# Holding back the first step of a gather until stages of another chain are done

## The chip, the cores and the metric

The kernel runs on one core of a Trainium2 chip. TensorE multiplies matrices, VectorE and ScalarE work elementwise, GpSimd (POOL in the profile) issues the indirect gathers, and SyncE (SP) issues most loads. The metric is the time of one execution in microseconds (us); of several runs the median is given. Lower is better.

## What is computed

A decoder block over 512 tokens with a model width of 1024: a normalized input goes through two token mixers in parallel (attention and a recurrent mixer, RWKV-7), their outputs are merged by gates, and the result goes through a channel mixer that picks 128 of 16384 experts for each token.

```python
h = modulate(rms_norm(x, norm_mix), sh1, sc1)
mix = token_mixer(h, ...)            # (g_mla * o_mla + g_rwkv * o_rwkv) @ w_out
x = x + gt1 * mix
h = modulate(rms_norm(x, norm_ffn), sh2, sc2)
# peer_ffn: top 16 of two lists of 128 keys for each of 8 heads, top 16 of their sums
act = gelu(einsum('bpd,bphkd->bphk', h, expert_down[expert_idx]))
x = x + gt2 * einsum('bphk,bphkd->bpd', gates * act, expert_up[expert_idx])
```

In the recurrent mixer each head's output is normalized over its 64 channels (the group norm of the title's chain), gets a bonus term, and is multiplied by a gate.

## The kernel before

The 512 tokens are four blocks of 128 rows. They go through the block's stages in three groups: block 0, block 1, and blocks 2 and 3 together; this third one is the last group. The code is a set of generators that emit instructions; a list scheduler then fixes one order for each engine, by a simulated time and a priority (`tc.cur_priority`), and on the chip each engine works through its order without leaving it. An engine that waits for one instruction holds up all that stand behind it.

The channel mixer is done in two ways. For blocks 0 and 1 it is done by **gathers**, in `peer()`: 128 per block, 256 in all. Gather number s fetches, for each of the 128 tokens, one expert's row of `expert_down` and one of `expert_up` into a tile gl of 128 x 2048 (1.05 MB; L1116, issued by GpSimd; four gl buffers, GL). VectorE's first step (L1119) multiplies gl's lower half with the token's row h2p and adds up into z. ScalarE takes gelu(z) and multiplies it with the gate (L1120, L1121). VectorE's second step (L1125) adds z times gl's upper half to acc. The second step frees the gl buffer, and only then can the gather four numbers later be issued. At the end of a block acc is multiplied and added with two rows e (L1131, L1132) and stored to out (L1133, issued by SP); the next block then loads h2p (L1109) and clears acc on GpSimd (L1111), and both have a single buffer. The gathers are emitted at the back of the priority (LATE), so the scheduler puts them into gaps.

For blocks 2 and 3 all experts are computed **densely**. Their chain, the last group's, is: `rwkv_out` (the group norm from the reduce m, L879, to y*m, L887; the transposition into ps_ynT, L893; bonus and gate, L903 and L904, up to the two products yT, L906), `tail_b` (ps_m = w_o times yT on TensorE, then Gr and Mg on VectorE, L953 and L954), `tail_c` (ps_mix = Mg times w_out; t_mix and x, L977 and L978; the norm of the rows and x*rs, L986; the transposition into ps_h2T, L991; h2T and its split hh and hl, L1148 and L1149; then ps_q = h2T times w_q and the top-16 search, from L1014), the selection, `dense_spread` (o and og, L1234 and L1237, build the gate matrix, which goes through the memory tile gd and comes back as G), and the dense loop of 128 iterations. An iteration splits u_raw and v_raw into high and low parts (uh, ul, vh, vl, L1148 and L1149), computes ps_z and accumulates into acc on TensorE (a PSUM tile of the same name as the gathers' acc), and multiplies act with G (L1287). At its end y = acc * gt + x2e (L1310, L1311) is stored to out.

The gathers run beside the last group's chain, the spread and the dense loop, and use the same VectorE, ScalarE and DMA engines.

Of the kernel before, what the change touches and what calls it, by code (L numbers as in the profile page):

```python
# [2 lines left out]

# [5 lines left out]
F32 = mybir.dt.float32  # L10
# [6 lines left out]
ALU = mybir.AluOpType  # L17
AX = mybir.AxisListType

P = 128  # L20
T = 512
D = 1024
# [12 lines left out]
LATE = 1000  # L35
ZLATE = 100
ZFIRST = 20
AZ = 32
PZ = 8
NG = 3  # L40
# [113 lines left out]
def _build(ctx, tc, nc, A, out):  # L154
# [309 lines left out]
    for ct in range(4):  # L464
        st = sp.tile([P, 2, 64], F32, name="st", tag="st", bufs=8)
        G.memset(st, 0.0)
        state.append(st)

    def norm(x, junk):

# [404 lines left out]
    def rwkv_out(cts, nb, R, y2, sg, yT):  # L875

        yv = y2.rearrange("p d (h c) -> p (d h) c", h=2)
        m, m2_, m3 = small("m", 4), small("m2", 4), small("m3", 4)
        V.tensor_reduce(m, yv, axis=AX.X, op=ALU.add)  # L879
        V.tensor_scalar(m, m, 1.0 / 64, None, op0=ALU.mult)  # L880
        V.tensor_tensor(yv, yv, bc(m, 64, 2), op=ALU.subtract)
        j = fin("jv", [P, 4, 64])
        S.activation(j, yv, AF.Square)
        V.tensor_reduce(m2_, j, axis=AX.X, op=ALU.add)
        V.tensor_scalar(m2_, m2_, 1.0 / 64, None, op0=ALU.mult)
        rsqrt(m3, m2_, 4, GN_EPS)
        V.tensor_tensor(yv, yv, bc(m3, 64, 2), op=ALU.mult)  # L887
        yield
        ps = psum_r("ps_ynT")
        u = fin("u", [P, 2, P])  # L890
        for d in range(2):
            ct = cts[d // nb]
            PE.transpose(ps[:, d * P:(d + 1) * P], y2[:, d], ident)  # L893
            S.activation(u[:, d], ps[:, d * P:(d + 1) * P], AF.Identity, scale=col("ln_x_w")[:, ct:ct + 1],
                         bias=col("ln_x_b")[:, ct:ct + 1])
        t = fin("bv", [P, 2, P])
        ps = psum_r("ps_bonus")
        mm(ps[:, :256], C("blk"), R["rk"])
        for d in range(2):
            mm(ps[:, 256 + d * P:256 + (d + 1) * P], w_gu[:, cts[d // nb] * P:(cts[d // nb] + 1) * P],  # L900
               sg[:, (d % nb) * P:(d % nb + 1) * P])
        yield
        V.tensor_tensor(flat(t), ps[:, :256], R["v"], op=ALU.mult)  # L903
        V.tensor_tensor(u, u, t, op=ALU.add)  # L904
        for d in range(2):
            V.tensor_tensor(yT[d % nb][:, cts[d // nb]], u[:, d], ps[:, 256 + d * P:256 + (d + 1) * P], op=ALU.mult)  # L906
        yield


# [27 lines left out]
    def tail_b(blocks, M, Gr, yT):  # L937
        nb = len(blocks)
        n = nb * P
        jn = 4 // nb  # L940
        for j0 in range(0, KT, jn):
            ps = psum_x("ps_m")
            for j in range(j0, j0 + jn):
                if j % 2 == 0:
                    w = load_w("w_o", A["w_o"][1, j // 2])
                for bb in range(nb):
                    o = ps[:, ((j - j0) * nb + bb) * P:((j - j0) * nb + bb + 1) * P]
                    for k in range(4):
                        mm(o, w[:, 4 * (j % 2) + k], yT[bb][:, k, :], k == 0, k == 3)
            pv = ps.rearrange("p (j b t) -> p b j t", j=jn, b=nb)  # L950
            for bb in range(nb):
                g, m = Gr[bb][:, j0:j0 + jn], M[bb][:, j0:j0 + jn]
                V.scalar_tensor_tensor(g, g, 1.0, pv[:, bb], op0=ALU.add, op1=ALU.mult)  # L953
                V.tensor_tensor(m, m, g, op=ALU.add)  # L954
            yield

    def tail_c(blocks, M, tops):
        nb = len(blocks)
# [22 lines left out]
        for bb, b in enumerate(blocks):  # L981
            nc.scalar.dma_start(x2d[b * P:(b + 1) * P, :], x2[bb])
            hT2 = (hTr if b in DENSE else Mh)("h2T", [P, KT, P])
            h2T.append(hT2)
            rs = norm(x2[bb], flat(hT2))
            V.tensor_scalar(x2[bb], x2[bb], rs, None, op0=ALU.mult)  # L986
            for k4 in range(2):
                ps = psum_x("ps_h2T")
                for j in range(4):
                    k = 4 * k4 + j  # L990
                    PE.transpose(ps[:, j * P:(j + 1) * P], x2[bb][:, k * P:(k + 1) * P], ident)  # L991
                for j in range(4):
                    k = 4 * k4 + j
                    S.activation(hT2[:, k], ps[:, j * P:(j + 1) * P], AF.Identity, scale=hA2[:, k:k + 1], bias=hB2[:, k:k + 1])
            if b in DENSE:
                dense_h(b, hT2)
                if b == DENSE[-1]:
                    ahead["z"] = dense_ahead()
            yield
        for bb, b in enumerate(blocks):  # L1000
# [101 lines left out]


    LAG = 1

    def peer(b, ii, gates, pl):

        h2 = pl.tile([P, D], F32, name="h2p", tag="h2p", bufs=1)
        nc.sync.dma_start(h2, h2d[b * P:(b + 1) * P, :])  # L1109
        acc = pl.tile([P, D], F32, name="acc", tag="acc", bufs=1)  # L1110
        G.memset(acc, 0.0)  # L1111
        wait = []
        for s in range(P + LAG):
            if s < P:
                gl = pl.tile([P, 2 * D], F32, name="gl", tag="gl", bufs=GL)
                G.indirect_dma_start(out=gl, out_offset=None, in_=A["experts"],  # L1116
                                     in_offset=bass.IndirectOffsetOnAxis(ap=ii[:, s:s + 1], axis=0))
                z = pl.tile([P, 2], F32, name="z", tag="z", bufs=4)
                V.scalar_tensor_tensor(gl[:, :D], gl[:, :D], 1.0, h2, op0=ALU.mult, op1=ALU.mult, accum_out=z[:, 0:1])  # L1119
                S.activation(z[:, 1:2], z[:, 0:1], AF.Gelu_apprx_tanh)  # L1120
                S.activation(z[:, 1:2], z[:, 1:2], AF.Copy, scale=gates[:, s:s + 1])  # L1121
                wait.append((gl, z))
            if s >= LAG:
                gl, z = wait.pop(0)
                V.scalar_tensor_tensor(acc, gl[:, D:], z[:, 1:2], acc, op0=ALU.mult, op1=ALU.add)  # L1125
            if s % 2:
                yield
        e = pl.tile([P, 2, D], F32, name="e", tag="gl", bufs=GL)
        nc.sync.dma_start(e[:, 0], mrow[3:4, :].to_broadcast([P, D]))
        nc.sync.dma_start(e[:, 1], x2d[b * P:(b + 1) * P, :])  # L1130
        V.tensor_tensor(acc, acc, e[:, 0], op=ALU.mult)  # L1131
        V.tensor_tensor(acc, acc, e[:, 1], op=ALU.add)  # L1132
        nc.sync.dma_start(out[b * P:(b + 1) * P, :], acc)  # L1133
        yield
# [11 lines left out]

    def hi_lo(hi, lo, x):
        S.copy(hi, x)  # L1148
        V.tensor_tensor(lo, x, hi.bitcast(F32), op=ALU.subtract)  # L1149

    def dense_open():
        dn["z"] = dz = pool("dz")
# [4 lines left out]
    def dense_h(b, h2T):  # L1157
        q = DENSE.index(b)
        S.copy(dn["hf"][:, :, q * P:(q + 1) * P], h2T)
        hi_lo(*(t[:, :, q * P:(q + 1) * P] for t in dn["h"]), h2T)  # L1160

    def dense_z(i):

# [295 lines left out]
```

## Time and profile before

| | us |
| --- | --- |
| median of 3 runs | 1945.18 |
| lowest and highest run | 1934.06, 1948.34 |
| the profiled execution | 1931.73 |
| its span, first to last instruction | 1930.0 |

The profile is of one execution. Its page gives busy time by engine and by line; the table of windows gives busy time, mean granted TensorE clock (as a share of full speed), DMA share and GB/s by stretch; the timeline gives each instruction with its start, its length, and in brackets how long its engine had been idle and what ended the wait; the chain of waits is followed back from the last instruction. Times within the span are from its start.

### The profile page before, as it was taken

The page shows a single profiled execution, that of the slowest core. Times are in us where ns is not written, and L with a number is a line of the kernel's source. Part 1 is how long each engine was busy: PE and PEld are TensorE (multiplying, and loading weights), DVE is VectorE, ACT ScalarE, POOL GpSimd, SP SyncE. Part 2 cuts the span into 40 slices and gives each one's busy share as a digit, 9 for nine tenths or more (in the row PEclk, how much of TensorE's full clock was granted, in tenths as well). Part 3 has the DMA queues.
Part 4 walks back from the last instruction along what each step waited for, and adds up shares of the span by engine and source line. Part 5 has one row for each costly group of instructions (what it writes and reads, how often), then busy time and mean ns, then how long its engine had stood idle before and what let it go on. Part 6 is the DMA issues. An engine that isn't in the chain of part 4 may idle for free.

```text
span 1930.0 us, 30268 instructions
## 1 busy us (share of the span) xinstructions
PE 1712.6 (89%) x11002; PEld 1465.1 (76%) x11002; DVE 1597.4 (83%) x3724; ACT 702.8 (36%) x1727; POOL 447.9 (23%) x394
## 2 busy tenths in 40 slices
PE   2889999999899999994769868978899999999998
PEld 2667777778787798883458857766689989988897
DVE  6675546458778898887789999977899999999997
ACT  1244233321323322231131123343465555555553
POOL 1210010000232200333322224310133433233230
PEclk9999999899999999996989988998999999999999
DMA  7744755166987975988989978998999999999995
GB/s 299 261 155 146 240 171 181 33 222 211 371 334 266 346 237 180 337 307 301 372 346 354 342 286 307 364 343 331 404 382 404 415 413 415 416 415 413 415 398 201
DMA packets 152642, 595.03 MB, mean 308 GB/s; under 512 B 13854, under 2 KB 47902, under 8 KB 117548
## 3 DMA queue, kind: packets, MB, share of 16 engines
q1 hardware_dynamic: 76768, 287.22, 40.3%
q0 software_dynamic: 39360, 280.51, 37.7%
q10 hardware_dynamic: 36364, 25.36, 4.2%
q8 instruction: 86, 1.41, 0.3%
q14 instruction: 64, 0.52, 0.1%
HBM read 569.96 MB, written 23.09 MB: 307 GB/s over the span
## 4 chain that ended last, share of the span: by engine, by line
issue 31%; PE 28%; DMA 14%; POOL 13%; DVE 12%; ACT 1%; POOLq 0%; SPq 0%; DVEq 0%; ACTq 0%
POOL gl L1116 13%; DMA gl<-in_experts,ii 6%; PE ps_b L234 4%; PE ps_q L234 3%; DMA w_b<-in_w_b 3%; PE ps_gt L234 3%; DVE acc L1125 2%; DVE gl L1119 2%; DMA w_out<-in_w_out 2%; PE ps_m L234 2%; PE ps_ap L234 2%; PE ps_mix L234 2%; DMA w_ada<-in_w_ada 2%; PE ps_y L234 1%; PE ps_s L234 1%
## 5 line engine op out<-in xcount | busy, mean ns | idle before, releaser
L1116 POOL DMA_INDIRECT gl<-in_experts,ii x256 | 393.6, 1537 | 988.5 <-DVE acc L1125 727.1
L1119 DVE SCALAR_TENSOR_TENSOR gl<-gl,h2p 128x1024 f32<-128x1024 f32 x256 | 311.2, 1216 | 51.6 <-DMA gl<-in_experts,ii 51.2
L1125 DVE SCALAR_TENSOR_TENSOR acc<-gl,z,acc 128x1024 f32<-128x1024 f32 x256 | 326.5, 1275 | 5.8 <-ACT z L1121 5.1
L234 PE MATMUL acc<-vh,ch 128*128 128x512 f32 x512 | 198.0, 395 | 11.1 <-ACT ch L1148 9.8
L234 PE MATMUL acc<-vl,ch 128*128 128x512 f32 x512 | 203.0, 397 | 4.3 <-DVE vl L1149 4.3
L234 PE MATMUL acc<-vh,cl 128*128 128x512 f32 x512 | 203.8, 398 | 2.6 <-DVE cl L1149 2.4
L234 PE MATMUL ps_z<-hh,ul 128*128 128x256 f32 x704 | 199.5, 283 | 2.4 <-DVE ul L1149 2.4
L234 PE MATMUL ps_z<-hh,uh 128*128 128x256 f32 x704 | 199.4, 283 | 0.4 <-ACT act L1188 0.4
L234 PE MATMUL ps_z<-hl,uh 128*128 128x256 f32 x704 | 199.6, 283 | 0.0
L1120 ACT ACTIVATE z<-z 128x1 f32<-128x1 f32 x256 | 51.9, 203 | 389.1 <-DVE gl L1119 389.0
L234 PE MATMUL ps_z<-hf,u_raw 128*128 128x256 f32 x640 | 160.2, 391 | 12.6 <-ACT i1T L1222 12.6
L1149 DVE TENSOR_TENSOR vl<-v_raw,vh 128x1024 fp32r<-128x1024 f32 x128 | 156.1, 1219 | 7.8 <-ACT vh L1148 7.6
L234 PE MATMUL ps_gt<-hT,w_b 128*128 128x128 f32 x1024 | 135.2, 285 | 9.8 <-DMA w_b<-in_w_b 7.3
L234 PEld LDWEIGHTS ps_z<-hf,u_raw 128*128 128x128 f32 x640 | 116.9, 195 | 31.6 <-ACT i1T L1222 13.0
L1148 ACT CAST vh<-v_raw 128x1024 fp32r<-128x1024 f32 x128 | 134.1, 1048 | 16.2 <-DMA v_raw<-in_dense 10.1
L234 PEld LDWEIGHTS ps_z<-hh,uh 128*128 128x128 f32 x704 | 134.6, 191 | 7.0 <-issue 3.1
L234 PEld LDWEIGHTS ps_gt<-hT,w_b 128*128 128x128 f32 x1024 | 126.0, 199 | 16.2 <-issue 11.1
L234 PEld LDWEIGHTS ps_z<-hl,uh 128*128 128x128 f32 x704 | 134.8, 192 | 3.1
L234 PEld LDWEIGHTS ps_z<-hh,ul 128*128 128x128 f32 x704 | 134.7, 191 | 2.7 <-DVE ul L1149 2.6
L234 PE MATMUL ps_b<-hT,w_b 128*128 128x128 f32 x896 | 123.2, 287 | 13.9 <-DMA w_b<-in_w_b 11.0
L234 PEld LDWEIGHTS ps_b<-hT,w_b 128*128 128x128 f32 x896 | 112.5, 199 | 24.4 <-issue 12.8
L234 PE MATMUL ps_q<-h2T,w_q 128*128 128x128 f32 x1024 | 125.5, 277 | 1.2 <-DMA w_q<-in_w_query 1.1
(432 smaller groups left out, 3308.5 us busy)
## 6 DMA issues: line engine op xcount, KB each, us to landing
u_raw<-in_dense SPq DMA_DIRECT2D x128, 512.0 KB
v_raw<-in_dense SPq DMA_DIRECT2D x128, 512.0 KB
w_b<-in_w_b SPq DMA_DIRECT2D x90, 512.0 KB
w_q<-in_w_query SPq DMA_DIRECT2D x48, 512.0 KB
w_ada<-in_w_ada SPq DMA_DIRECT2D x32, 512.0 KB
G<-gd SPq DMA_DIRECT2D x16, 1024.0 KB
w_o<-in_w_o SPq DMA_DIRECT2D x24, 512.0 KB
w_out<-in_w_out SPq DMA_DIRECT2D x24, 512.0 KB
```

The source lines that it names most:

```text
L234: PE.matmul(o, l, r, start=start, stop=stop)
L1116: G.indirect_dma_start(out=gl, out_offset=None, in_=A["experts"], in_offset=bass.IndirectOffsetOnAxis(ap=ii[:, s:s + 1], axis=0))
L1119: V.scalar_tensor_tensor(gl[:, :D], gl[:, :D], 1.0, h2, op0=ALU.mult, op1=ALU.mult, accum_out=z[:, 0:1])
L1120: S.activation(z[:, 1:2], z[:, 0:1], AF.Gelu_apprx_tanh)
L1125: V.scalar_tensor_tensor(acc, gl[:, D:], z[:, 1:2], acc, op0=ALU.mult, op1=ALU.add)
L1148: S.copy(hi, x)
L1149: V.tensor_tensor(lo, x, hi.bitcast(F32), op=ALU.subtract)
```

## The change

A function `meter(n, ins)` notes an instruction and a number. `metered(n)` gives the context `tc.issue_after` for the latest note whose number is at most n, or an empty context. Three instructions of the last group's chain are noted: the last product into yT (73), the last addition into Mg (77) and the subtraction that makes hl of block 3 (83). The gathers' first VectorE steps, counted over both blocks from 0 by `taken`, are put behind these: numbers 73 to 76 behind yT, 77 to 82 behind Mg, all from 83 on behind hl. Only the first step is placed; the gather's DMA, ScalarE's steps and the second VectorE step carry no placement of their own. `issue_after` fixes the order among VectorE's instructions. `hi_lo` and `dense_h` now return the subtraction.

```diff
+METER = dict(mixed=73, merged=77, normed=83)
...
+    gates_at = []
+
+    def meter(n, ins):
+
+        assert not gates_at or gates_at[-1][0] <= n
+        gates_at.append((n, ins.ins))
+
+    def metered(n):
+        g = [i for c, i in gates_at if c <= n]
+        return tc.issue_after(g[-1]) if g else nullcontext()
...
         for d in range(2):
-            V.tensor_tensor(yT[d % nb][:, cts[d // nb]], u[:, d], ps[:, 256 + d * P:256 + (d + 1) * P], op=ALU.mult)
+            last = V.tensor_tensor(yT[d % nb][:, cts[d // nb]], u[:, d], ps[:, 256 + d * P:256 + (d + 1) * P],
+                                   op=ALU.mult)
+        if nb > 1 and cts[-1] == 3:
+            meter(METER["mixed"], last)
         yield
...
-                V.tensor_tensor(m, m, g, op=ALU.add)
-            yield
+                last = V.tensor_tensor(m, m, g, op=ALU.add)
+            yield
+        if nb > 1:
+            meter(METER["merged"], last)
...
             if b in DENSE:
-                dense_h(b, hT2)
+                last = dense_h(b, hT2)
                 if b == DENSE[-1]:
+                    meter(METER["normed"], last)
                     ahead["z"] = dense_ahead()
...
     LAG = 1
+    taken = [0]
...
-                V.scalar_tensor_tensor(gl[:, :D], gl[:, :D], 1.0, h2, op0=ALU.mult, op1=ALU.mult, accum_out=z[:, 0:1])
+                with metered(taken[0]):
+                    V.scalar_tensor_tensor(gl[:, :D], gl[:, :D], 1.0, h2, op0=ALU.mult, op1=ALU.mult,
+                                           accum_out=z[:, 0:1])
+                taken[0] += 1
```

The scheduler takes the new constraints into account, so the order of VectorE changes from there to the end of the program. The changed kernel's lines have other numbers: a gather's first step is L1140, its second L1148, the closing steps L1154 and L1155, y L1333 and L1334. A row of these listings gives line, operation, out<-in and size.

The first place is the end of the last group norm, on VectorE, up to yT and the steps behind it. Before:

```order
L887 TENSOR_TENSOR y_6747<-y_6747,m_7401 128x256
L1125 SCALAR_TENSOR_TENSOR acc<-gl,z,acc 128x1024
L1119 SCALAR_TENSOR_TENSOR gl,z<-gl,h2p 128x1024
L903 TENSOR_TENSOR bv<-ps_bonus,sh 128x256
L1125 SCALAR_TENSOR_TENSOR acc<-gl,z,acc 128x1024
L904 TENSOR_TENSOR u<-u,bv 128x256
L1119 SCALAR_TENSOR_TENSOR gl,z<-gl,h2p 128x1024
L906 TENSOR_TENSOR yT<-u,ps_bonus 128x128 x2
L1125 SCALAR_TENSOR_TENSOR acc<-gl,z,acc 128x1024
L1119 SCALAR_TENSOR_TENSOR gl,z<-gl,h2p 128x1024
```

And of the change, the same place:

```order
L900 TENSOR_TENSOR y_6747<-y_6747,m_7401 128x256
L916 TENSOR_TENSOR bv<-ps_bonus,sh 128x256
L917 TENSOR_TENSOR u<-u,bv 128x256
L919 TENSOR_TENSOR yT<-u,ps_bonus 128x128 x2
L1140 SCALAR_TENSOR_TENSOR gl,z<-gl,h2p 128x1024 x2
L1148 SCALAR_TENSOR_TENSOR acc<-gl,z,acc 128x1024
L969 SCALAR_TENSOR_TENSOR Gr<-Gr,ps_m 128x256 x2
```

The gather steps that stood between the chain's steps are gone from there and begin behind yT.

The second place is the end of the spread, on VectorE, in the changed kernel alone; in the kernel before the two closing steps of block 0 and the first gather of block 1 stand some 130 to 160 rows earlier, in the selection.

```order
L1140 SCALAR_TENSOR_TENSOR gl,z<-gl,h2p 128x1024
L1257 TENSOR_TENSOR o_9768<-iota,i1T 128x1024
L1257 TENSOR_TENSOR o_9794<-iota,i2T 128x1024
L1260 TENSOR_TENSOR og<-o_9768,gb 128x1024 x2
...
L1257 TENSOR_TENSOR o_9865<-iota,i1T 128x1024
L1154 TENSOR_TENSOR acc<-acc,e 128x1024
L1260 TENSOR_TENSOR og<-o_9865,gb 128x1024 x2
L1172 TENSOR_TENSOR ul<-u_raw,uh 128x1024
L1155 TENSOR_TENSOR acc<-acc,e 128x1024
```

Its first row is the first step of gather 128, the first of block 1, which reads the new h2p.

The third place is the end of the program on VectorE. Before, the last rows are these (only y and the branch at the end follow):

```order
L1131 TENSOR_TENSOR acc<-acc,e 128x1024
L1149 TENSOR_TENSOR ul<-u_raw,uh 128x1024
L1287 SCALAR_TENSOR_TENSOR act<-act,G 128x256
L1132 TENSOR_TENSOR acc<-acc,e 128x1024
L1149 TENSOR_TENSOR cl<-act,ch 128x256
L1149 TENSOR_TENSOR vl<-v_raw,vh 128x1024
```

Of the change, from the last y on; 18 rows of the same alternation are left out:

```order
L1334 TENSOR_TENSOR y<-y,x2e 128x512 x2
L1148 SCALAR_TENSOR_TENSOR acc<-gl,z,acc 128x1024
L1140 SCALAR_TENSOR_TENSOR gl,z<-gl,h2p 128x1024
...
L1148 SCALAR_TENSOR_TENSOR acc<-gl,z,acc 128x1024
L1154 TENSOR_TENSOR acc<-acc,e 128x1024
L1155 TENSOR_TENSOR acc<-acc,e 128x1024
```

Ten first steps, twelve second steps and the closing steps of block 1 now stand behind the last y. GpSimd's order is the same in both.

## Rows read from the trace of the kernel before

**Rows 1.** The page, part 1: busy us (share of span), instructions.

```profile
PE 1712.6 (89%) x11002; PEld 1465.1 (76%) x11002; DVE 1597.4 (83%) x3724; ACT 702.8 (36%) x1727; POOL 447.9 (23%) x394
```

**Rows 2.** Windows: length, then busy us (count) by engine, PEclk, DMA share, GB/s.

```profile
891.85:915.67 23.82, 2.54 (x9) 1.83 (x9) 22.15 (x45) 5.01 (x19) 11.94 (x8) 0.50 0.75 272
...
933.74:972.20 38.46, 30.04 (x66) 12.22 (x64) 26.26 (x35) 3.98 (x16) 11.92 (x9) 0.96 1.00 406
972.20:1003.50 31.30, 14.17 (x95) 13.27 (x95) 28.05 (x58) 15.43 (x41) 10.89 (x8) 0.73 0.84 314
1003.50:1131.40 127.90, 120.44 (x790) 111.06 (x789) 122.45 (x507) 23.05 (x79) 29.93 (x26) 0.99 0.92 341
...
1500.00:1600.00 100.00, 99.39 (x633) 90.02 (x632) 98.86 (x130) 55.53 (x111) 40.93 (x20) 1.00 1.02 414
```

The engines in Rows 2 are, in this order, PE, PEld, DVE, ACT and POOL.

**Rows 3.** Windows of L1119 alone (first gather steps), on DVE.

```profile
891.85:915.67 23.82, 8.64 (x14) 0.50 0.75 272
...
972.20:1003.50 31.30, 9.81 (x16) 0.73 0.84 314
```

**Rows 4.** Windows of L1125 alone (second gather steps), on DVE.

```profile
891.85:915.67 23.82, 10.23 (x8) 0.50 0.75 272
...
972.20:1003.50 31.30, 10.36 (x9) 0.73 0.84 314
```

**Rows 5.** Timeline of PE: start, us, instruction, [idle before <-what ended it].

```profile
909.58 0.47 PE L893 MATMUL ps_ynT<-cst,y 128*128 128x128 f32 x1 [18.07 <-DVE y L887]
...
928.46 5.44 PE L234 MATMUL ps_m<-yT,w_o 128*128 128x128 f32 x32 [2.27 <-DMA w_o<-in_w_o]
...
946.97 5.09 PE L234 MATMUL ps_mix<-w_out,Mg 128*128 128x512 f32 x8 [2.77 <-DMA w_out<-in_w_out]
954.50 3.67 PE L234 MATMUL ps_mix<-w_out,Mg 128*128 128x512 f32 x8 [2.44 <-DMA w_out<-in_w_out]
961.32 10.90 PE L234 MATMUL ps_mix<-w_out,Mg 128*128 128x512 f32 x24 [3.15 <-DMA w_out<-in_w_out]
983.09 1.97 PE L991 MATMUL ps_h2T<-cst,x 128*128 128x128 f32 x8 [10.88 <-DVE rsg L273]
990.69 1.97 PE L991 MATMUL ps_h2T<-cst,x 128*128 128x128 f32 x8 [5.63 <-DVE x L986]
```

**Rows 6.** Timeline of DVE, an early group's norm, first and last step.

```profile
331.32 0.42 DVE L879 TENSOR_REDUCE m<-y 128x4 f32<-128x256 f32 x1 [1.25 <-ACT y L872]
...
346.33 0.29 DVE L906 TENSOR_TENSOR yT<-u,ps_bonus 128x128 f32<-128x128 f32 x1
```

**Rows 7.** The page, part 5: busy us, mean ns, idle before and releaser.

```profile
L1119 DVE SCALAR_TENSOR_TENSOR gl<-gl,h2p 128x1024 f32<-128x1024 f32 x256 | 311.2, 1216 | 51.6 <-DMA gl<-in_experts,ii 51.2
L1125 DVE SCALAR_TENSOR_TENSOR acc<-gl,z,acc 128x1024 f32<-128x1024 f32 x256 | 326.5, 1275 | 5.8 <-ACT z L1121 5.1
```

**Rows 8.** Timeline of POOL: the block change, and a gather in the spread.

```profile
1148.79 0.95 POOL L1111 MEMSET acc<- 128x1024 f32 x1 [8.80 <-DMA out<-acc]
...
1171.08 4.08 POOL L1116 DMA_INDIRECT gl<-in_experts,ii  x1 [12.38 <-DVE acc L1125]
```

**Rows 9.** Timeline of DVE: a pair's wait, the spread's end, the final y.

```profile
948.38 1.28 DVE L1125 SCALAR_TENSOR_TENSOR acc<-gl,z,acc 128x1024 f32<-128x1024 f32 x1 [0.60 <-ACT z L1121]
...
1285.65 1.29 DVE L1237 TENSOR_TENSOR og<-o,gb 128x1024 f16<-128x1024 f16 x2
...
1312.15 1.09 DVE L1287 SCALAR_TENSOR_TENSOR A<-A,G 128x256 f32<-128x256 f32 x3 [5.14 <-DMA G<-gd]
...
1921.13 1.37 DVE L1310 TENSOR_TENSOR y<-acc,gt 128x512 f32<-128x512 f32 x2 [1.69 <-PE acc L234]
```

**Rows 10.** The chain that ended last: a gather's transfer (start, us).

```profile
993.24 6.51 DMA gl<-in_experts,ii
```

More of the change, by code (lines that the diff above doesn't have):

```diff
@@ L2 @@
 import math
-from contextlib import ExitStack
+from contextlib import ExitStack, nullcontext
 import numpy as np
@@ L1148, in hi_lo @@
         S.copy(hi, x)
-        V.tensor_tensor(lo, x, hi.bitcast(F32), op=ALU.subtract)
+        return V.tensor_tensor(lo, x, hi.bitcast(F32), op=ALU.subtract)
     def dense_open():
@@ L1159, in dense_h @@
         S.copy(dn["hf"][:, :, q * P:(q + 1) * P], h2T)
-        hi_lo(*(t[:, :, q * P:(q + 1) * P] for t in dn["h"]), h2T)
+        return hi_lo(*(t[:, :, q * P:(q + 1) * P] for t in dn["h"]), h2T)
     def dense_z(i):
```

## The prediction

> **What bounds the kernel now.** I read the page's busy shares first: TensorE 89%, VectorE 83% of the span [rows 1]. Such shares average over stages, so I cut the trace into stretches with the table of windows. From 1500 to 1600 us, in the dense loop, TensorE is busy 99.4 of 100 us, VectorE 98.9, and the DMA engines are full (share 1.02, 414 GB/s) [rows 2]. Three resources are at their limit at once there, and nothing is to be had from moving work within it. The last group's chain looks otherwise. From 891.85 (the m reduce of the last group norm) to 915.67 (end of yT) TensorE works 2.54 of 23.82 us while VectorE works 22.15 [rows 2]. From 972.2 (the last added halves of x) to 1003.5 (the first top-16 step) TensorE works 14.17 of 31.3 and VectorE 28.05 [rows 2]. In these two stretches VectorE decides, and most of what it does there belongs to the gathers: in the first 8.64 (seven first steps, two records each) and 10.23 us (eight second steps), in the second 9.81 and 10.36 us [rows 3, 4]. The timeline of TensorE shows the same from the other side: its first matmul behind the group norm starts after 18.07 us of waiting for VectorE's y, and the first transposition of the normalized rows after 10.88 [rows 5].
>
> **The tasks that move.** No operation is added or removed. Gathers 73 to 76 may take their first step only behind yT, 77 to 82 behind the last added Mg, all later ones behind hl of block 3. Counted in the order of VectorE, before has done 81 first and 80 second steps at the end of yT, 100 and 98 at hl, and 256 and 256 when the final y begins; after has 73 and 73, 83 and 83, and 246 and 244. So ten first and twelve second steps, then block 1's closing acc*e, acc+e and store, stand behind the final y, where before had all of them ahead of it. The sum is therefore: what the chain gains, minus a tail behind y, plus small terms between.
>
> *Group norm to yT.* Without the 18.87 us of gather steps [rows 3, 4], 4.95 us of VectorE's own work is left [rows 2 to 4], and the waits of a dependent chain through ScalarE and TensorE become visible. VectorE idled only 23.82 - 22.15 = 1.67 us before. An early group, ahead of any gather, took from 331.32 to 346.62 for the same steps, 15.3 us, with other work between them [rows 6]. That gives a gain of 8 at least; with nothing but the chain's own work, 1.67 of idle and some 2.5 us of newly visible latency I get 9.1, a gain of 14.7, and at most 16. I take 14.7, nearer the upper end, because here hardly any foreign step is left in the order.
>
> *w_o and w_out.* TensorE waits once 2.27 us for w_o and 2.77 + 2.44 + 3.15 = 8.36 for w_out [rows 5]. The gathers compete for the same DMA engines, which are full from 933.74 to 972.2 (share 1.00, [rows 2]), and fewer of them (10 first steps in place of 26 between m and hl) leave room; but the same transfers are now also wanted earlier. From 0 to 2.27 for the first, from 0 to 8.36 for the second; I take 2.3 and, for what hinges on room in the DMA engines, two thirds, 5.5.
>
> *x to the first top-16 step.* 31.3 us, of which 20.17 are gather steps [rows 3, 4]; TensorE's own 14.17 and the norm's dependent steps stay. TensorE's two waits, for the two blocks' rows, were 10.88 and 5.63 us [rows 5], 16.5 together, and about 11 of that are gather steps and their waits; the rest is the norm's own. Bounds 8 and 12, taken 11. The chain in all: 14.7 + 2.3 + 5.5 + 11 = 33.5, rounded 33 (20 to 38).
>
> *Top-16 and dense loop.* Between the first and the last top-16 step 27 first steps stand in the order of VectorE, before and after, and between the first and the 124th vl of the dense loop 110, before and after. In the first TensorE is busy 120.44 and VectorE 122.45 of 127.9 us, in the second three resources are full [rows 2]: these stretches keep their length, 0. In the last four iterations after has five first steps, before none: TensorE paces there (y waits for it 1.69 us [rows 9]), and five gathers on a VectorE with idle time cost 0 to 5, taken 3.
>
> *Spread.* The change from block 0 to block 1 moves from the selection to the end of the spread. VectorE's steps between the last top-16 step and the first vl stay equal in number (18 first and 16 second ones before, 17 and 17 after, acc*e and acc+e in both). But the first gather of block 1 now stands among the og steps with h2p, a 512 KB load, issued shortly ahead of it: a wait of 0 to the 8.80 us that POOL waited for a 512 KB store [rows 8]; behind it are queued the og steps on which TensorE waits. I take +3, near the lower end, since some 5 us of o and og steps lie between (0 to 9). The memset behind the same store holds up VectorE's next acc, but between the last og (1285.65) and the first A<-A,G (1312.15) VectorE waits for gd to come back anyway, 26.5 us [rows 9]; without that cover it would cost some 6.
>
> *The tail.* Two first and four second steps alternate freely: 2 x 1.23 + 4 x 1.20 = 7.3 (1.216 and 1.275 us each in the table of lines [rows 7], which overlap by some 0.07). Then eight pairs where a gather's second step stands right behind its own first: 1.15 + 0.08 + 0.60 for ScalarE's two steps on z (the wait that such a pair shows [rows 9]) + 1.20 = 3.03 each, 24.2. Last 2 x 1.14 for acc*e and acc+e. Sum 33.8. Would transfers pace it? A slot is used again after POOL's 2.05 us (40.93 us for 20 gathers [rows 2]), 6.51 for the transfer [rows 10], 1.2 + 0.6 + 1.2 on the two engines: 11.6 for four slots, 2.9 per gather, under 3.03. At 414 GB/s ten gathers of 1.05 MB are 25 us, less than the tail. So 33.5, no less than the bare 10 x 1.23 + 12 x 1.20 + 2.3 = 29 and 38 if each pair takes half a microsecond more. The store behind it costs what the store of y costs today.
>
> **Sum**: -33 + 0 + 3 + 3 + 33.5 = +6.5 us. The profiled execution took 1931.73 us with a span of 1930.0; that becomes about 1938.2. The median of the runs shown is 1945.18 and the profiled one is near their lowest (1934.06), so I add the same to the median: 1951.7.
>
> **Weighing a rule.** In the spread POOL takes 4.08 us for a gather while VectorE runs two-input steps back to back, in the loop 2.05 [rows 8, 2]. The Trainium skill, page "SBUF — State Buffer", section "Who interferes with whom", says that VectorE and GpSimd share one port pair as an exclusive lock, and that a queue whose descriptors GpSimd writes is starved of port time by VectorE; by that rule the tail, all gathers and VectorE steps, could run at the slow figure and the sum would come out at about +15. The row of the dense loop, the same two kinds of step beside the same gathers, speaks for 2.05, so the sum goes by that.
>
> **Rivals.** *The chain is paced by its latencies, not by the gathers (slower).* The dependent steps of the group norm and the row norm might need nearly all their time for themselves, VectorE merely being filled between them. The early group's 15.3 us [rows 6] speaks for it, the idle time of only 1.67 us against it. Then the chain saves 8 + 0 + 0 + 8 = 16, and -16 + 3 + 3 + 33.5 = +23.5, on the median 1968.7. The turning point is a chain saving of 20 us: below it the result is over 1% slower. *The dense loop speeds up (faster).* It has full DMA engines, and ten gathers (10.5 MB, 25 us at 414 GB/s) leave it for the tail, where TensorE no longer needs the DMA engines. If DMA alone set the loop's pace, the sum would be 6.5 - 25 = -18.5 or, with the chain's upper end, -23: about 1924. Against it: the order has 110 first steps in the loop as before, and those now behind y were taken out of the chain. *The tail is paced by POOL.* At 4.08 us a gather [rows 8] eight gathers take 33 in place of 24, and the sum is +15: 1960. *The order does nothing*, if the cores were to wait for w_out and w_o anyway: then only the tail counts, which is the slower rival in its extreme (+39.5, 1984.7).
>
> **How the numbers follow.** My forecast (+6.5, with the chain between 26 and 38) has 60 of 100, its own range -2 to +16. The latency rival has 18, POOL's pace 10, the loop's speed-up 8, the extreme 4. About 1% (19.5 us) is what a measurement of this kernel can tell from no change. Of the forecast's 60, nearly all is within that; the latency rival lies just beyond it, with 16 of 18 slower; POOL's pace within for 7 of 10 and the extreme beyond. So slower 0.24, faster 0.09, same 0.67. The range takes in the lower bounds -38 + 0 + 0 + 29 = -9, widened toward the faster rival to -19, and the upper -20 + 9 + 5 + 38 = +32, cut to +31: 1926 to 1976, which leaves out half of the faster rival and the extreme.
>
> **What would show each step.** Right: the first top-16 step near 970; the wait ahead of ynT's transposition near 6 us; y ending near 1899; then some 33 us in which TensorE stands still and VectorE alternates the two gather steps. Wrong: a first top-16 step later than 984 (latency rival), a y earlier than 1885 (the loop gained), a tail over 40 us (POOL or transfers pace it), or over 10 us of VectorE waiting for h2p or the memset near the spread's end.

## The result, and the profile after the change

The changed kernel takes 1948.91 us in the median, the kernel before 1938.82 on the same chips; the ratio is 1.006 with a 95% interval of 1.0041 to 1.0079. That is about 11.6 us more: a real loss, and under 1%. The profiled execution took 1948.5 us, with a span of 1946.7. It reached the m reduce of the last group norm 4.81 us later than that of before (896.66 in place of 891.85), although hardly anything differs up to there; in experiments 3 and 8, whose order up to there is that of before, it came at 904.70 and 890.09, so this is scatter. Most of the 16.7 us between the two spans, 11.9, lies behind this step: from m to the end it took 1050.04 us in place of 1038.15, which agrees with the ratio. So the stages are counted from m.

The windows of after, first those that answer to [rows 2] (length, busy us of PE, PEld, DVE, ACT and POOL, PEclk, DMA share, GB/s), then the dense loop and what follows the final y:

```profile
896.66:905.79 9.13, 2.54 (x9) 1.84 (x9) 5.44 (x24) 1.33 (x3) 0.00 (x0) 0.50 0.44 178
905.79:920.06 14.27, 14.27 (x110) 14.27 (x111) 12.32 (x23) 1.99 (x8) 2.62 (x2) 0.85 0.55 191
920.06:965.55 45.49, 33.71 (x66) 13.38 (x64) 21.82 (x32) 3.61 (x13) 8.52 (x8) 0.89 0.89 345
965.55:985.80 20.25, 15.15 (x95) 14.44 (x96) 12.05 (x36) 12.73 (x29) 0.00 (x0) 0.75 0.36 115
985.80:1118.99 133.19, 124.63 (x787) 113.82 (x787) 124.81 (x514) 22.64 (x78) 26.87 (x28) 0.95 0.88 319
...
1294.71:1901.31 606.60, 597.20 (x3522) 523.95 (x3523) 593.32 (x805) 329.81 (x648) 178.25 (x113) 1.00 1.00 403
...
1906.19:1942.85 36.66, 0.00 (x0) 0.00 (x0) 29.39 (x34) 4.97 (x20) 13.03 (x8) 0.51 0.77 285
```

Two windows of before that the rows ahead of the prediction don't have, cut at the same steps as the third and sixth row above (from the first ps_mix to the last x, and the dense loop):

```profile
933.74:974.68 40.94, 30.05 (x66) 12.22 (x64) 28.74 (x40) 5.12 (x18) 13.06 (x10) 0.96 1.00 406
...
1312.15:1921.13 608.98, 599.45 (x3527) 526.33 (x3528) 584.11 (x792) 327.58 (x636) 179.67 (x106) 0.99 0.98 390
```

From the windows of both, cut at the same steps:

| stretch | before | after | change | forecast |
| --- | --- | --- | --- | --- |
| m to yT | 23.82 | 9.13 | -14.7 | -14.7 |
| yT to the first ps_mix | 18.07 | 14.27 | -3.8 | -2.3 |
| first ps_mix to the last x | 40.94 | 45.49 | +4.5 | -5.5 |
| last x to the first top-16 step | 28.83 | 20.25 | -8.6 | -11 |
| top-16 stage | 129.95 | 133.19 | +3.2 | 0 |
| selection, spread, wait for G | 178.69 | 175.72 | -3.0 | +3 |
| dense loop | 608.98 | 606.60 | -2.4 | +3 |
| final y | 4.96 | 4.88 | -0.1 | 0 |
| behind y, with the store | 3.91 | 40.51 | +36.6 | +33.5 |
| sum | 1038.15 | 1050.04 | +11.9 | +6.5 |

(The forecast had the chain rounded to 33, hence 6.5 where its terms give 6.0. Its fourth stretch began 2.5 us earlier, at 972.2.)

Not every row of this table is a finding. Up to the dense loop, experiments 3 and 8 below have the order of before and experiments 4 and 11 that of after, and their executions show how much a stretch varies by itself:

| stretch | before; 3; 8 | after; 4; 11 |
| --- | --- | --- |
| m to yT | 23.82; 23.92; 23.82 | 9.13; 9.14; 9.13 |
| yT to the first ps_mix | 18.07; 15.86; 15.46 | 14.27; 14.27; 14.41 |
| first ps_mix to the last x | 40.94; 42.88; 40.61 | 45.49; 41.92; 43.41 |
| last x to the first top-16 step | 28.83; 29.64; 31.89 | 20.25; 21.45; 19.76 |
| top-16 stage | 129.95; 127.70; 129.06 | 133.19; 125.36; 134.82 |
| selection, spread, wait for G | 178.69; 178.22; 177.22 | 175.72; 182.89; 177.10 |

The first and the fourth stretch shrink whichever two are compared. The row of the spread does not stand out from its scatter, and neither does that of the loop, which took 603.81 us in experiment 8 (the order of before) and 609.12 in experiment 4 (that of after). From m to the first top-16 step the chain saves 22.5 us in the pair of profiles shown, and 22.5 to 25.6 over all pairs.

The rows of TensorE that answer to [rows 5], its timeline in the chain:

```profile
901.88 0.47 PE L906 MATMUL ps_ynT<-cst,y 128*128 128x128 f32 x1 [5.55 <-DVE y L900]
...
930.05 5.37 PE L236 MATMUL ps_mix<-w_out,Mg 128*128 128x512 f32 x8 [2.96 <-DMA w_out<-in_w_out]
939.50 5.37 PE L236 MATMUL ps_mix<-w_out,Mg 128*128 128x512 f32 x8 [4.08 <-DMA w_out<-in_w_out]
947.02 12.23 PE L236 MATMUL ps_mix<-w_out,Mg 128*128 128x512 f32 x24 [2.16 <-DMA w_out<-in_w_out]
961.08 3.70 PE L236 MATMUL ps_mix<-w_out,Mg 128*128 128x512 f32 x8 [1.83 <-DMA w_out<-in_w_out]
969.45 1.97 PE L1009 MATMUL ps_h2T<-cst,x 128*128 128x128 f32 x8 [4.67 <-DVE ss L487]
972.62 1.97 PE L1009 MATMUL ps_h2T<-cst,x 128*128 128x128 f32 x8 [1.20 <-DVE x L1004]
```

TensorE's wait ahead of the first transposition fell from 18.07 to 5.55 us, those ahead of the rows' transpositions from 10.88 and 5.63 to 4.67 and 1.20. Its waits for w_out grew from 8.36 in all to 11.03. Behind the final y VectorE's timeline shows the work that came there:

```profile
1904.91 1.28 DVE L1334 TENSOR_TENSOR y<-y,x2e 128x512 f32<-128x512 f32 x2
...
1918.08 1.23 DVE L1140 SCALAR_TENSOR_TENSOR gl<-gl,h2p 128x1024 f32<-128x1024 f32 x1 [0.66 <-DMA gl<-in_experts,ii]
1919.23 0.08 DVE L1140 DVE_READ_ACCUMULATOR gl<-gl,h2p 128x1 f32 x1
1919.91 1.28 DVE L1148 SCALAR_TENSOR_TENSOR acc<-gl,z,acc 128x1024 f32<-128x1024 f32 x1 [0.60 <-ACT z L1144]
...
1941.63 1.22 DVE L1155 TENSOR_TENSOR acc<-acc,e 128x1024 f32<-128x1024 f32 x1
```

Eight such pairs stand there, each with the wait of 0.60 us for ScalarE, and four of them wait 0.25 to 0.84 us more for their transfer.

One more view sums it up: the windows from m to the end, first of before, then of after.

```profile
891.85:1930.00 1038.15, 916.68 (x5580) 793.62 (x5580) 958.40 (x1734) 441.57 (x949) 302.78 (x181) 0.95 0.95 366
```

```profile
896.66:1946.70 1050.04, 920.24 (x5580) 794.10 (x5580) 960.92 (x1735) 442.03 (x949) 289.33 (x180) 0.94 0.94 363
```

VectorE is busy 958 and 961 us of that, so it is the fullest engine behind m, and the loss is for the most part (9.4 of 11.9 us) idle time of VectorE: 79.8 us before, 89.1 after. The chain up to the first top-16 step has VectorE idle 37.5 us after the change (9.13 + 14.27 + 45.49 + 20.25 less the busy times in the windows above); before it was some 23.

### The profile page after: what moved, and what is told of

It reads as the page before. It is cut to its first block, busy times and chain, and to the rows that moved or that the text cites. A ratio compares the mean times of both kernels' runs of the same rounds, so it can differ in the third digit from the quotient of the medians.

```text
span 1946.7 us, 30278 instructions
## 1 busy us (share of the span) xinstructions
PE 1719.2 (88%) x11002; PEld 1469.9 (76%) x11002; DVE 1600.0 (82%) x3724; ACT 703.2 (36%) x1727; POOL 436.5 (22%) x394
## 3 DMA queue, kind: packets, MB, share of 16 engines
q0 software_dynamic: 39360, 280.51, 37.5%
## 5 line engine op out<-in xcount | busy, mean ns | idle before, releaser
L1136 POOL DMA_INDIRECT gl<-in_experts,ii x256 | 381.4, 1490 | 1050.2 <-DVE acc L1148 744.2
L1140 DVE SCALAR_TENSOR_TENSOR gl<-gl,h2p 128x1024 f32<-128x1024 f32 x256 | 311.2, 1216 | 48.6 <-DMA gl<-in_experts,ii 48.3
L1148 DVE SCALAR_TENSOR_TENSOR acc<-gl,z,acc 128x1024 f32<-128x1024 f32 x256 | 326.5, 1275 | 11.8 <-ACT z L1144 11.0
L236 PE MATMUL ps_gt<-hT,w_b 128*128 128x128 f32 x1024 | 136.3, 287 | 11.3 <-DMA w_b<-in_w_b 11.2
```

What stands on the lines that cost most here:

```text
L236: PE.matmul(o, l, r, start=start, stop=stop)
```

## Experiments

All ratios are to the kernel before, timed on the same chip as the experiment.

**1. The first gate alone.** What of the loss is due to which gate? The rows of METER for Mg and hl are dropped; `meter` notes only what has a number.

```diff
-METER = dict(mixed=73, merged=77, normed=83)
+METER = dict(mixed=73, merged=None, normed=None)
...
+        if n is not None:
```

> The change with its first gate alone: gathers from 73 on stand behind yT, the gates at Mg and hl are gone. In the order of VectorE one first and two second steps are left behind the final y, in place of ten and twelve. Theory 'VectorE's work is conserved' (the traces of before and after: VectorE busy 958 and 961 us from the m reduce to the end, the time differs by its idle time alone): the stage from m to yT still shrinks from 23.8 to about 9 us with only 2 us more idle time, the dense loop takes the deferred steps into its idle time (25 us before, 13 after), the tail is about 7 us. Sum -14.8 + 2 for the work that lands in the chain + 7 in the tail: about -6 to -10 us against before, ratio 0.995. Rival 'one for one' (each of the eight deferred gathers comes back at the tail's price of 3 us somewhere before the end): -14.8 + 24 = +9, ratio 1.005.

Measured: ratio 0.9998 (0.9965 to 1.003), between the two forecasts, and the interval takes in neither. Windows of this kernel: m to yT, first ps_mix to the last x, last x to the first top-16 step, dense loop:

```profile
897.67:906.80 9.13, 2.54 (x9) 1.83 (x9) 5.44 (x24) 1.33 (x3) 0.43 (x1) 0.51 0.67 267
...
921.36:967.39 46.03, 32.84 (x66) 13.45 (x64) 29.85 (x41) 5.62 (x20) 12.15 (x11) 0.89 0.98 385
967.39:998.50 31.11, 17.49 (x110) 16.38 (x111) 25.82 (x55) 14.46 (x39) 9.11 (x7) 0.73 0.83 312
...
1307.46:1921.10 613.64, 601.94 (x3530) 526.39 (x3531) 594.35 (x806) 330.80 (x648) 205.78 (x113) 0.99 0.99 398
```

The first stretch is 14.7 us shorter, as in after; yet from m to the end the profiled execution took 1041.13 us, 3 more than before. The gathers held back there run in the next stretches and in the loop (VectorE busy 594 us in it, 584 before), and the time comes back in those.

**2. A gate at hl alone.**

```diff
-METER = dict(mixed=73, merged=77, normed=83)
+METER = dict(mixed=None, merged=None, normed=93)
...
+        if n is not None:
```

> One gate alone, at hl of block 3, with the number 93 that before has reached there by itself when the last rows of x are summed: gathers from 93 on stand behind hl; the gates at yT and Mg are gone. Two first and three second steps are left behind the final y. In after this stretch (x to the first top-16 step) shrank by 10.3 us and VectorE's idle time in it rose from 3.25 to 8.28. Conserved work: -10 in the chain, a tail of about 10 us (2 first, 3 second, two closing steps), loop unchanged: 0 +- 4 us against before, ratio 1.000. One for one: -10 + 7 x 3 = +11, ratio 1.006.

Measured: ratio 1.0008 (0.9983 to 1.0033), the number of conserved work. The stretch from the last x to the first top-16 step, and the loop:

```profile
985.57:1010.82 25.25, 14.79 (x95) 14.08 (x96) 12.15 (x37) 13.22 (x29) 0.18 (x1) 0.73 0.47 170
...
1312.11:1927.43 615.32, 601.38 (x3523) 524.73 (x3524) 593.20 (x805) 328.85 (x647) 227.27 (x114) 0.99 0.99 396
```

The first of them is 3.6 us shorter than before (28.83), where after gained 8.6. So the terms of that forecast did not come: from m to the first top-16 step the chain took 106.32 us (111.66 before), 5 less and not 10, and the loop 615.32, 6 more and not as long as before. That the number came out is in part luck. From m to the end the two single gates take 1041.13 and 1040.30 us with VectorE busy 959 in both. Neither gate alone gains or loses what can be measured.

**3 and 4. Ten gathers left out, before and after.** Is the chain's gain real, and does the dense loop wait for VectorE? Both kernels compute 118 of block 1's 128 gathers.

```diff
-        for s in range(P + LAG):
-            if s < P:
+        own = P - 10 if b == 1 else P
+        for s in range(own + LAG):
+            if s < own:
```

> The kernel before with the last ten gathers of block 1 left out (118 in place of 128; that part of the output is then not computed). Everything ahead of the loop's end is as before. If the dense loop is paced by TensorE (busy 599 of 609 us), taking 24 us of VectorE's work and 25 us of transfers out of it changes the time by 0 to -6 us. If VectorE or the DMA engines pace it, by -18 to -25 us.

> The changed kernel with the same ten gathers left out, which are the ten first steps behind the final y. Both theories: the tail of 36.7 us shrinks to two second and two closing steps, about 5 us, so -31 us against after and -20 against before. What tells the theories apart is the comparison with the shortened kernel before: with a loop paced by TensorE the chain's gain of 20 to 24 us remains between the two shortened kernels; if VectorE or the DMA engines pace the loop, the shortened before is some 20 us faster as well and the two are within 6 us of each other.

Measured: the shortened before 0.9949 (0.9912 to 0.9986), about -10 us; the shortened after 0.9847 (0.9803 to 0.9891), about -30. The loop of the shortened before:

```profile
1322.92:1934.33 611.41, 600.88 (x3527) 525.69 (x3528) 563.02 (x761) 322.92 (x616) 171.54 (x96) 0.99 0.95 374
```

VectorE works 21 us less in it than before, and it still lasts 611 us with TensorE busy 601: in this execution TensorE paces it. Both kernels came out some 10 us below their forecasts (0 to -6, and -20). The interval of the first, about -3 to -17 us, leaves out the -18 to -25 of a loop paced by VectorE or the DMA engines, but where those 10 us come from the profiles do not say. Between the two shortened kernels 20 us of the chain's gain remain, with some 11 us either way (an estimate from the two intervals), where a loop paced by VectorE or the DMA engines would have left under 6. The gain is thus real, and the changed kernel loses it behind y.

**5 and 11. Filling the loop.** Can the ten gathers go into the dense loop, whose VectorE is idle 13 us in after? The scheduler's priority is changed.

```diff
-LATE = 1000
+LATE = 0        # fifth;  LATE = 100 in the eleventh
```

> The changed kernel with LATE 0 in place of 1000: the gathers' instructions are no longer at the back of the scheduler's priority in the dense loop. Up to hl and through the spread VectorE's order stays as in after; in the loop VectorE now does all 256 first and 255 second steps, so only one second and the two closing steps stand behind the final y. Theory 'two limits' (the loop lasts as long as TensorE needs, 605 to 611 us, until VectorE's own work, 593 us in after, exceeds it): the 22 us that come back make VectorE's work 615, so the loop takes about 618 (+11), the tail falls from 36.7 to about 4: -21 against after, m reduce to end about 1028, ratio to before 0.994. Rival 'tail price': a gather step placed ahead of ul, vl or cl holds TensorE up by its full length wherever it stands, so the loop grows by 30 us or more and the time stays at after's, ratio 1.006 or above.

> The changed kernel with LATE 100, between the 1000 of after and the 0 of the fifth experiment: six first and seven second steps are left behind y (after: ten and twelve; fifth experiment: none and one). So four first and five second steps, 11 us of VectorE's work, come into the dense loop. Full price (the loop's VectorE is already busy 593 of 607 us, and what is put in beside that costs as much as in the tail): the loop grows by 12 to 16 us, the tail falls from 36.7 to about 22, the time stays within 3 us of after, ratio to before 1.005 to 1.007. Free filling (the 13 us that VectorE is idle in after's loop take the work in): the loop stays at 607 to 611, -12 us against after, ratio 0.999.

Measured: 1.005 (1.0023 to 1.0078) and 1.0049 (1.0022 to 1.0076), both as after, so the theory of two limits and the free filling fell, and the time is that of the tail price and the full price. Loop and tail of the eleventh:

```profile
1298.45:1923.70 625.25, 604.52 (x3525) 526.12 (x3526) 604.56 (x820) 332.39 (x658) 189.31 (x117) 0.99 1.00 398
...
1928.58:1950.64 22.06, 0.00 (x0) 0.00 (x0) 18.30 (x21) 2.98 (x12) 4.30 (x3) 0.50 0.64 244
```

The tail lost 14.6 us, and the loop of this execution grew by 18.7 with 11.2 more of VectorE's work in it. By the ratios the two kernels differ by 2 us, with some 6 either way (an estimate from both intervals), so that the loop grew by about 12.5: the work costs about its own length there, and that it costs more is not shown. TensorE's waits in the eleventh's loop show where much of it comes from (groups by line, of the loop: count, busy us, mean ns, idle before and its releasers); in after the idle time of this group was 6.0 us, 3.4 of it for ch:

```profile
L236 PE MATMUL acc<-vh,ch 128*128 128x512 f32 x511 | 196.8, 397 | 15.2 <-ACT ch L1171 11.6 <-ACT vh L1171 3.4
```

An iteration's chain runs from act on VectorE over ch on ScalarE to acc on TensorE. The added gather steps stand in it, mostly in the last iterations. The last tenth of the loop, first of after, then of the eleventh:

```profile
1840.65:1901.31 60.66, 60.05 (x376) 53.79 (x375) 60.11 (x81) 31.24 (x67) 20.07 (x13) 1.00 0.94 366
```

```profile
1861.18:1923.70 62.52, 50.90 (x281) 42.24 (x280) 57.73 (x79) 26.57 (x61) 18.83 (x15) 0.95 0.89 336
```

TensorE is busy nearly all the time in the first and idle for 11.6 us in the second. Whether an even spread of these steps over all iterations would be cheaper was not tried.

**6 and 8. The first gate with LATE 0, and before with LATE 0.**

```diff
-LATE = 1000
+LATE = 0        # both
...
-METER = dict(mixed=73, merged=77, normed=83)
+METER = dict(mixed=73, merged=None, normed=None)        # sixth alone
```

> The gate at yT alone (as in the first experiment) and LATE 0: one second step and the closing steps are left behind y, as nearly all were before. Two limits: its loop with LATE 1000 was 613.6 us with VectorE busy 594; 1 first and 2 second steps come into it: loop 614 to 618, tail 4: within 4 us of the first experiment, ratio 0.998. Tail price: the same, as hardly a step moves; this run shows what LATE 0 does by itself to the order of the loop.

> The kernel before with LATE 0, as the control for the two runs with LATE 0. All its gathers end ahead of y already, and its loop is paced by TensorE. Two limits: 0 +- 3 us against before, ratio 1.000. Tail price: steps taken earlier in the loop hold TensorE up: +5 to +15, ratio 1.003 to 1.008.

Measured: 0.9972 (0.9945 to 0.9999) and 0.9995 (0.9962 to 1.0028). In before LATE 0 leaves the order of VectorE, TensorE, GpSimd and SyncE as it was, instruction by instruction. So experiment 8 is in effect a second run of before, and it can't tell two limits from the tail price; what it shows is the scatter. With the one gate at yT and a tail of 3.7 us behind y the kernel is 0.3% faster than before in the ratio; the interval ends at one, and it overlaps that of experiment 1.

**7. No gather from the last Mg to hl.** What makes the waits for w_out?

```diff
-METER = dict(mixed=73, merged=77, normed=83)
+METER = dict(mixed=73, merged=None, normed=77)
...
+        if n is not None:
```

> The change without its middle: gathers 73 to 76 behind yT, all from 77 on behind hl (77 in place of 83), so that no gather step, and after the four buffers are full no gather transfer, stands between the last Mg and hl. 21 first and 23 second steps are left behind y (after: ten and twelve). Theory 'transfers' (w_out's waits of 8.4 us before and 11.0 after come from DMA engines at 350 to 406 GB/s shared with gathers and u_raw): the waits fall below 4 us in all and the stretch from the first ps_mix to the last x from 45.5 to about 36. Rival 'lead' (three w2 buffers let each w_out be requested too late, whatever else is moved): the waits stay at 8 to 11 us and the stretch at 43 or more. The time in all: the chain gains 6 to 10 us more, the tail grows by 11 x 3.3 = 36: +28 against after, ratio to before 1.020.

Measured: ratio 1.0134 (1.0105 to 1.0163). The waits fell to 3.82 us, and the stretch to 34.39, as transfers had it, and the rival 'lead' fell; the tail behind y grew to 68.2 (timeline of TensorE, all its waits for w_out; then the two windows):

```profile
931.12 5.37 PE L236 MATMUL ps_mix<-w_out,Mg 128*128 128x512 f32 x8 [2.23 <-DMA w_out<-in_w_out]
938.08 17.41 PE L236 MATMUL ps_mix<-w_out,Mg 128*128 128x512 f32 x40 [1.59 <-DMA w_out<-in_w_out]
```

```profile
921.86:956.25 34.39, 29.80 (x66) 12.38 (x64) 7.46 (x13) 0.62 (x1) 1.87 (x2) 0.95 0.76 274
...
1899.10:1967.30 68.20, 0.00 (x0) 0.00 (x0) 55.99 (x67) 10.44 (x42) 32.22 (x19) 0.50 0.85 316
```

Eleven gathers more in the tail cost 31.5 us there, 2.87 each (3.3 was foreseen). The total was some 13 us under its forecast of 1.020; about 5 of them are the tail's. The chain up to the first top-16 step gained 11.5 us on after where 6 to 10 were foreseen; the rest is open.

**9 and 10. Loads of u_raw behind w_out.** SP had put four loads of u_raw, which the dense part needs, between those of w_out. In after (timeline of SP, which issues them):

```profile
920.69 1.56 SPq L1198 DMA_DIRECT2D u_raw<-in_dense  x2
923.69 0.33 SPq L985 DMA_DIRECT2D w_out<-in_w_out  x1
924.07 0.43 SPq L1198 DMA_DIRECT2D u_raw<-in_dense  x1
927.13 0.33 SPq L985 DMA_DIRECT2D w_out<-in_w_out  x1
927.50 0.44 SPq L1198 DMA_DIRECT2D u_raw<-in_dense  x1
935.45 17.30 SPq L985 DMA_DIRECT2D w_out<-in_w_out  x3
```

They are placed behind the last w_out, in the sixth experiment's kernel and in before.

```diff
...
+                if nb > 1:
+                    held["w_out"] = wo.ins     # the DMA of w_out
...
+        with tc.issue_after(held["w_out"]) if i < 4 else nullcontext():
             nc.sync.dma_start(u, A["dense"][i, 0])
```

> The sixth experiment's kernel (gate at yT alone, LATE 0), and the first four loads of u_raw (2.1 MB), which SP had put between those of w_out, are placed behind the last w_out. Transfers: the waits for w_out, 10.6 us in the sixth experiment, fall to about 5 (2.1 MB at 380 GB/s are 5.5 us), the stretch from the first ps_mix to the last x from 46.9 to about 41; what VectorE does not do there it does no later than the loop, so -4 us in all against the sixth experiment, ratio to before 0.995. Rival 'passed on': u_raw then competes with w_q in the next stretch, which grows by as much as was gained: ratio 0.997 as in the sixth.

> The kernel before with the same four loads of u_raw placed behind the last w_out, as the control. Its waits for w_out were 8.4 us. Transfers: they fall to about 4 and the time by 0 to 4 us, ratio 0.998 to 1.000. Passed on: ratio 1.000 to 1.003.

Measured: 0.9977 (0.9951 to 1.0003) and 1.0022 (0.9986 to 1.0057). The waits for w_out fell to 3.85 and 2.57 us, and the next stretch took it back. First ps_mix to the last x and the stretch after it, in the sixth and the ninth:

```profile
924.97:971.91 46.94, 33.85 (x66) 13.84 (x64) 29.92 (x40) 5.63 (x20) 12.13 (x11) 0.85 0.98 379
971.91:1000.90 28.99, 16.27 (x100) 15.43 (x101) 25.85 (x57) 14.35 (x39) 8.46 (x7) 0.65 0.84 304
```

```profile
923.69:962.83 39.14, 30.09 (x66) 12.31 (x64) 29.97 (x43) 5.62 (x20) 13.46 (x11) 0.94 0.98 393
962.83:997.30 34.47, 18.06 (x113) 16.89 (x114) 25.99 (x57) 14.58 (x39) 8.81 (x7) 0.68 0.90 346
```

7.8 us less, then 5.5 more: passed on, all but some 2 us, which the ratios can't tell from nothing. No version that computes all gathers beats before by more than its interval, except the sixth by a hair; among eleven experiments that can be chance.

## Why the prediction held, step by step

The direction, the size class and the main mechanism were right: +0.6% measured, +0.3% forecast (6.5 of 1945 us), inside the range and inside 1%. A chain that gains, and a tail behind y that costs more, is what the traces show. The sizes fit less well. The chain saved 22.5 us in place of 33, less than the 26 that the forecast took as its least, and the top-16 stage and the tail cost 3 us more each. The total came near because the 6 us charged to the spread and the loop did not come (-5.4 in the table, inside the scatter). That it lies within 5 us of the forecast is in part luck. One sign that was to show the latency rival did appear: the first top-16 step came at 985.80, later than 984; counted from m, which came 4.81 us later, it is 980.99. The prediction also held that about 1% is the least that a measurement can tell from no change; with the runs taken here the interval is 0.2% either way, and 0.6% is outside it.

- **Group norm to yT**: -14.7 forecast, -14.7 measured; a stage of 9.1 us. The working behind it has two errors that cancel. The 4.95 us that it takes for VectorE's own work are 23.82 less 18.87, so they hold the idle time of 1.67, which it then adds once more; what [rows 2 to 4] leave of busy time is 3.28. In after VectorE's own steps take 5.44 us, more than that remainder, because neighbouring steps overlap (a step of 1.28 us that starts at 912.46 is followed by one at 913.66) and the windows of single lines count the overlap twice; the idle time is 3.69, of which 2.49 is the wait for ps_bonus. The 2.5 us of newly visible latency were thus right. The idle time of 1.67 us in the row of before was the telling number: an interval in which an engine hardly idles shrinks by what is taken from that engine, until the waits of the chain itself come out.
- **w_o**: -2.3 forecast, -3.8 measured, of which the other executions of these orders bear out 1 to 2.
- **w_out**: the step that failed. I let fewer gathers end two thirds of the waits; they grew by 2.7 us. Over the executions in the table they are 8.36, 9.52 and 7.75 before and 11.03, 9.94 and 9.57 after, so nowhere did they fall. TensorE was also busy 3.7 us longer for the same 64 matmuls. Experiment 7 shows that competition of transfers was the right mechanism: with no gather in the stretch the waits fall to 3.8. What was mis-sized is the competition left: in after POOL still issues eight gathers there (ten before), and experiment 9 shows four loads of u_raw in the same stretch. The chain arrived earlier, and the DMA engines had nearly as much to bring (by their rates an estimate of 15.7 MB in 45.49 us, 16.6 MB in 40.94), though with a share of 0.89 they were not full all through. TensorE's longer work goes with a lower granted clock, 0.89 in place of 0.96 [rows 2]; the clock was 0.92 and 0.84 in experiments 4 and 11, with the same order, and 0.95 in experiment 7, whose order there lacks only the gathers. Why it was lower is not settled.
- **x to the top-16 step**: -11 forecast for 31.3 us; 8.6 measured for a stretch that begins 2.5 us later. Near enough.
- **Top-16 and loop**: 0 and +3 forecast, +3.2 and -2.4 measured. The loops of before and of experiments 8 and 10, whose order there is the same, last 604 to 609 us, so the second is no finding. The first probably is one. I put it at nothing because as many gather steps stand in this stage before and after; their order differs, though. With the order of after the stage took 133.19 us, and 133.80 and 134.82 in experiments 7 and 11, at a clock of 0.95 or 0.96; with that of before 129.95, and 127.70, 129.06 and 129.02 in experiments 3, 8 and 10, at 0.97 to 0.99. But experiment 4 has the order of after and took 125.36 at 0.99. So the longer time goes with a lower granted clock of TensorE, mostly but not always with the new order, and what lowers the clock is open.
- **Spread**: the wait for h2p that I charged 3 us did not happen. In after's timeline the first step of gather 128 stands among the og steps without a wait, and VectorE waited for a gather's transfer (7.98 us) only behind the last og, under the cover of G, which came 26.5 us behind the last og as before. The -3.0 of the stretch is inside its scatter.
- **Tail**: 33.5 forecast, 36.6 measured. The count of ten, twelve and two steps and the 0.60 us per pair were right; the missing 3 us are mostly the four waits for transfers, 2.3 us in all. I had set the transfers at 2.9 us a gather against 3.03 for the pair and called that enough; it was too near.

The rivals: the **latency rival** did not come, since both stretches shrank almost as forecast; but the chain as a whole saved 22.5 us, close to its turning point of 20, because of w_out. **POOL's pace** fell: POOL issues the gathers of the tail in 0.94 to 1.94 us, beside VectorE's f32 steps with two inputs, and not in the 4.08 of [rows 8]:

```profile
1917.69 0.94 POOL L1136 DMA_INDIRECT gl<-in_experts,ii  x1 [1.34 <-DVE acc L1148]
1921.47 1.68 POOL L1136 DMA_INDIRECT gl<-in_experts,ii  x1 [2.84 <-DVE acc L1148]
```

The Trainium skill, page "SBUF — State Buffer", section "Who interferes with whom", which I weighed there, names VectorE's 2-port modes, and says of steps with two inputs in SBUF only that they contend with a GpSimd instruction that reads SBUF, a condition that I left out. By it GpSimd could have been slowed; the tail's rows don't show it. In the spread of after the slow figure is there again: eight gathers take 4.09 us and one 6.89. What makes the difference was not tested. **The loop's speed-up** fell too: taking ten gathers out of it (experiment 3) left it at 611 us, and the loop of after lasts as long as that of before.

One thing the prediction had half: it said that three resources are full in the loop. Taking VectorE's work out did not shorten it in the profile of experiment 3, and putting 11 us in lengthened it by about as much (experiment 11). Yet the loop of after holds 9 us more of VectorE's work than that of before and is no longer, 606.60 us and, in experiment 4, 609.12; in experiments 1 and 2 nearly as much of it goes with 613.64 and 615.32. So a part can be had for nothing, and where the steps stand counts; which places are free is open. What the tail shows is a price of VectorE's work behind y, about 3 us for a gather, and what was pushed from there into the loop cost about as much. Before, the seven first and eight second steps ahead of yT cost the chain 14.7 us, about 2 us for a gather, which is less.

## What to carry to other kernels

Holding work back from a critical stretch pays only if a later stage takes it up for less than the stretch gains; look for that stage first, and price the work there. Here the chain gained 22.5 us and the tail cost 36.6. Where one engine is busy for most of the time to the end (VectorE for 958 of 1038 us), compare the idle time of that engine before and after: a change that only moves its work can gain no more than the idle time that it fills, and here it added 9 us. A stretch that is sped up asks for its transfers earlier, so don't count on a wait for a DMA behind it to go away: the wait for w_out grew from 8.4 to 11.0 us. And run the same order more than once before a row of a few us is explained: the top-16 stage of one order took 125 to 135 us.

## What was not expected of the hardware

The granted clock of TensorE in the top-16 stage differed between executions of the same order (0.95 with 133.19 us, 0.99 with 125.36 us, in after and in experiment 4), as large an effect as most terms of the sum. The price of a gather's two steps depends on the loop that takes them: the first 9 us of VectorE's work that came into the dense loop with the change cost nothing that shows (VectorE busy 584 us before, 593 after), the next 11 us about their own length (18.7 us in one execution, some 12.5 by the ratios).
